# A hybrid HGRN2 and pooling decoder block in fp32: the order of the seven products of a pair, where the split operands begin, and the rooms of the pool's gates

## The chip, the core and the metric

The kernel runs on one core of a Trainium2 chip. Its five engines work side by side, each through its own list of instructions in order: TensorE (PE in the profile; its weight loads are listed apart as PEld), VectorE (DVE), ScalarE (ACT), GpSimd (POOL) and SyncE (SP), which here does nothing but issue transfers between DRAM and the on-chip memory. TensorE reads its two operands from the on-chip memory (SBUF) and writes its sums into eight accumulation banks (PSUM), from which VectorE and ScalarE read them. An instruction waits on semaphores for those of other engines that it depends on.

The metric is the device time of one execution in microseconds. Several executions of one kernel are given by their median. The profile is of one further execution; its span runs from the first to the last instruction.

## The reference

One decoder block over 1024 tokens of width 1024, all in fp32:

```python
def hybrid_mixer(x, w_in, lower_bound, hgrn_norm_g, w_a, w_pool, pool_scale, w_out):
    proj = x @ w_in                       # 1024 x 7168
    q, f_pre, i_val, o_gate, pool_v, gate_a, gate_b = jnp.split(proj, splits, axis=-1)
    ...
    o = hgrn2_chunked(q, 1 - f, i_val, log_f)        # 8 heads, a gated linear recurrence
    o = o * lax.rsqrt(jnp.mean(jnp.square(o), axis=-1, keepdims=True) + RMS_EPS)
    a = (o * hgrn_norm_g * jax.nn.sigmoid(o_gate)) @ w_a
    pooled = causal_multiscale_pool(pool_v)          # trailing means over 2, 4, 8, 16 tokens
    b = jnp.einsum('bsgc,gcd->bsgd', pooled, w_pool) * pool_scale
    merged = jax.nn.sigmoid(gate_a) * a + jax.nn.sigmoid(gate_b) * b
    return merged @ w_out

def sq_relu_mlp(x, w_up, w_down):
    return jnp.square(jax.nn.relu(x @ w_up)) @ w_down

x = layer_norm(ALPHA * x + hybrid_mixer(...));  x = layer_norm(ALPHA * x + sq_relu_mlp(x, w_up, w_down))
```

## The kernel before

**Three matmuls for one.** Every fp32 operand of a large product is split into a high part (rounded by a copy on ScalarE) and a low part (what is left, a subtraction on VectorE), and a product is the sum high x high + high x low + low x high: the three matmul lines 211, 213, 214 (and 112 to 114, 479 to 481, 1348 to 1350 in the other stages).

**Seven products for eight.** The products with w_in, w_a, w_up and w_down go through a scheme of Strassen and Winograd's kind. A *pair* (lines 266 to 353) is 256 output columns by 1024 tokens by 1024 deep, as 2 x 2 blocks b11, b12, b21, b22 of the weights. Seven operands are made from the blocks (b11, b21, T3 = b22 - b12, T4, T2, T1, b22), each is split into two w tiles (`w_part`, line 244, in lines 125 and 126; ring of ten, so five operands), and each meets one of seven activation operands that were split once and kept (`xp`: a11, a12, s3, a22, s2, s1, s4). A product is twelve matmuls of 128 x 512 (`prod`, line 206). Its sums go into banks: a takes P1, P6, P5, P3 one on top of the other; z takes P7, P4; c takes P2. Between these the sums so far are read: c11 = a after P1 (copied by ScalarE, line 274), c22 = z after P7, c21 = a after P6; P2 is added to c11, z (after P4) to c21, a (after P5) to c22 (VectorE, line 278), and a after P3 is the fourth block. `takes[0..3]` are what the pair's user does with the four results (sigmoid and store, pooling, squared ReLU). Ordinary banks are a ring of four (pj); z may lie in one of two others (hg, sc), c in tr.

**Order.** The steps of a pair stand in one tuple (line 350) as operand and product; `run` (line 357) makes the operands and issues the products of one pair, or of two pairs side by side (w_a, the first two pairs of w_up). With two side by side, a product of the one stands between two of the other; I call the others single pairs: 24 of w_in and 14 of w_up (the third of w_up has its first products among those of the two that run side by side). In the stage of w_in, from the pair after `head_inputs(0)` on, PE's order is the program's (`manual_schedule`, line 1016): after each product comes one step of the recurrence (`turning`, line 371), which is either nothing on PE, a few transposes and state products (lines 971, 937), or the large step of outputs, turned keys and scores (lines 955, 957, 894, 901, 912), once in 8.5 products. The other engines' order there, and every engine's elsewhere, is set when the program is built, by a planner that simulates the engines.

**Tiles.** Blocks of weights are loaded by SP (line 222, `loaded_blocks` line 230) into `raw`, a ring of six tiles, five for a pair of which "t" is scratch; results wait in `c` rooms (four on the left, two on the right). The tiles of the left side lie one behind another: constants (`const`, from line 134), two rings of statistics, then the 28 `act` tiles with the split activations, then `ca`. The w tiles, raw and two of the c rooms lie at the right end of the memory, where a filler of 96 bytes (line 82) sets where they begin, on a multiple of 128 bytes; with the sizes before them (const: ..., `prm` 128 bytes, `g_neg` 32, `lb` 32, `one_lb` 32, `e01` 64) the act tiles begin 32 bytes past one.

**Behind the recurrence** come four groups of `pool_products` (line 713: w_pool, its operands split into tiles of the tags q and f, four products each of six matmuls, a gate loaded for each from DRAM, multiplied in and stored again), the last gates, then w_a beside the loads of the recurrence's outputs, w_out, the first layer norm, w_up and w_down. Tags of the recurrence's rooms: q (three tiles), f (four), og (one), v (two).

Of the kernel before, what the change touches and what calls it, by code (L numbers as in the profile page):

```python
# [9 lines left out]
F32 = mybir.dt.float32  # L10
# [6 lines left out]
P = 128  # L17
# [3 lines left out]
KT = D // P  # L21
# [18 lines left out]
PRIO = 60  # L40
# [10 lines left out]
def tile_hybrid_block(  # L51
# [127 lines left out]
    def minus_sum(out, a, b):  # L179
        V.scalar_tensor_tensor(out, a, -1.0, b, ALU.mult, ALU.subtract)  # L180
# [25 lines left out]
    def prod(ps, w, name, first):  # L206
        wh, wl = w
        for k in range(CH):
            th, tl = xp[name][k][:, 0], xp[name][k][:, 1]
            with tc.high_priority(PRIO_WHOLE) if k else nullcontext():  # L210
                PE.matmul(ps, wh[:, k], th, start=first and k == 0, stop=False, skip_group_check=True)  # L211
            with tc.high_priority(PRIO_WHOLE):
                PE.matmul(ps, wh[:, k], tl, start=False, stop=False, skip_group_check=True)  # L213
                PE.matmul(ps, wl[:, k], th, start=False, stop=k == CH - 1, skip_group_check=True)  # L214
# [15 lines left out]
    def loaded_blocks(src, c1, c2, done=None):  # L230

        raw = {}
        for i in ((0, 0), (1, 0), (0, 1), "t", (1, 1)):
            raw[i] = block_tile(), None
            if i != "t":
                raw[i] = wide_block(src, i[0], (c1, c2)[i[1]], raw[i][0])
        if done is not None:
            done.append(raw[1, 1][1])
        return [raw[i][0] for i in ((0, 0), (0, 1), (1, 0), (1, 1), "t")]
# [4 lines left out]
    def w_part(src):  # L244
        return split(src, w_tile)
# [17 lines left out]
    def c_late():  # L263
        return c_tile(False)

    def pair(raw, rooms, takes, pz_tag="pj", pc_tag="pj", turned=False):


        b11, b12, b21, b22, t = raw if len(raw) == 5 else (*raw, None)
        c, ps = {}, {}  # L270

        def copied(room, ps):
            t = room()
            A.copy(t, ps)  # L274
            return t

        def added(t, ps):
            V.tensor_add(t, t, ps)  # L278
            return t

        def t3():
            c["t"] = block_tile() if t is None else t
            V.tensor_sub(c["t"], b22, b12)  # L283
            return w_part(c["t"])

        def t4():
            if turned:
                V.tensor_sub(b12, b11, b12)
                minus_sum(c["t"], b22, b12)
                minus_sum(b21, c["t"], b21)  # L290
            else:
                V.tensor_sub(b12, b12, b11)
                V.tensor_sub(c["t"], b22, b12)
                V.tensor_sub(b21, b21, c["t"])
            return w_part(b21)

        def t2():
            return w_part(c["t"])

        def t1():  # L300
            return w_part(b12)

        def p1(w):
            ps["a"] = ps_tile()
            prod(ps["a"], w, "a11", True)
            c[11] = copied(rooms[0], ps["a"])

        def p2(w):
            if pz_tag == "pj":
                ps["z"] = ps_tile()  # L310
            ps["c"] = ps_tile(pc_tag, 4 if pc_tag == "pj" else 2)
            prod(ps["c"], w, "a12", True)

        def p7(w):
            if pz_tag != "pj":
                ps["z"] = ps_tile(pz_tag, 2)
            prod(ps["z"], w, "s3", True)
            with tc.high_priority(PRIO):
                takes[0](added(c[11], ps["c"]))
                c[22] = copied(rooms[2], ps["z"])  # L320

        def p6(w):
            prod(ps["a"], w, "s2", False)
            with tc.high_priority(PRIO):
                c[21] = copied(rooms[1], ps["a"])
                takes[2](added(c[21], ps["z"]))

        def p4(w):
            prod(ps["z"], w, "a22", False)

        def p5(w):
            prod(ps["a"], w, "s1", False)
            with tc.high_priority(PRIO):
                takes[3](added(c[22], ps["a"]))

        def p3(w):
            prod(ps["a"], w, "s4", False)
            with tc.high_priority(PRIO):
                takes[1](ps["a"])

        def t0():
            return w_part(b11)

        def b_21():
            return w_part(b21)

        def b_22():
            return w_part(b22)

        return tuple(  # L350
            ((operand,), ((operand, product),))
            for operand, product in ((t0, p1), (b_21, p2), (t3, p7), (t4, p4), (t2, p6), (t1, p5), (b_22, p3))
        )

    turning = [iter(())]
# [46 lines left out]
    with tc.tile_pool(name="xr", bufs=8, side="right", reuse_waits="tile") as xr:  # L402
# [9 lines left out]
        PE.transpose(ps[:, 0:32], prm_r, ident[0:32, 0:32])  # L412
        V.tensor_copy(prm, ps[:, 0:32])
        g_col, pscale = prm[:, 16:24], prm[:, 24:32]
        g_neg = const.tile([P, 8], F32, name="g_neg")
        V.tensor_scalar_mul(g_neg, g_col, -1.0)
        lb = const.tile([P, 8], F32, name="lb")
        one_lb = const.tile([P, 8], F32, name="one_lb")
        e01 = const.tile([P, 16], F32, name="e01")
# [5 lines left out]
        V.reciprocal(lb, lb)  # L425
        V.tensor_mul(lb, lb, e01[:, 0:8])
        V.tensor_scalar(one_lb, lb, -1.0, 1.0, ALU.mult, ALU.add)
        x_rows = [xr.tile([P, CH, D], F32, name=f"x{u}", bufs=1) for u in range(2)]
        for t in range(8):
            r[t] = x_rows[t // CH][:, t % CH]  # L430
# [163 lines left out]
    def loaded(src, tile_of):  # L594
        t = tile_of()
        nc.sync.dma_start(out=t, in_=src)
        return t
# [25 lines left out]
    with tc.tile_pool(name="tmp", bufs=1, side="right", reuse_waits="tile") as tmp:  # L623
# [15 lines left out]
        def tt(tag, dtype=F32):  # L639
            pool = tmp if tag in ("q", "f", "og", "v") else hgp  # L640
            return pool.tile([P, HALF], dtype, tag=tag, name=nm(tag), bufs=RINGS.get(tag, 1))
# [70 lines left out]

        def pool_products(g):

            rooms = iter((lambda: tt("v"), c_tile, lambda: tt("f"), c_tile))
            raw = loaded(w_pool[g].rearrange("(k p) c -> p k c", p=P), lambda: block_tile((2, 2 * P)))
            pods = [[loaded(pod[2 * g + i][u], lambda: block_tile((HALF,))) for i in range(2)] for u in range(2)]
            parts = iter(("q", "f"))
            wh, wl = split(raw, lambda: tt(next(parts), F32R).rearrange("p (k c) -> p k c", c=2 * P))
            for u in range(2):  # L720
                pl = [split(pods[u][i], row_tile) for i in range(2)]
                for i in range(2):
                    w = slice(i * P, (i + 1) * P)
                    j = 2 * g + i
                    room = next(rooms)
                    t = room() if j == KT - 1 else loaded(gbd[j][u], room)
                    ps = ps_tile()
                    mm3(ps, [(wh[:, c, w], wl[:, c, w], *pl[c]) for c in range(2)])
                    if j == KT - 1:
                        A.activation(t, ps, AF.Copy, scale=pscale[:, j : j + 1])  # L730
                    else:
                        V.scalar_tensor_tensor(t, ps, pscale[:, j : j + 1], t, ALU.mult, ALU.mult)
                    nc.sync.dma_start(out=pbd[j][u], in_=t)
# [334 lines left out]
        def a_pair(p):  # L1068
            cols = 2 * p * P, (2 * p + 1) * P
            raw = loaded_blocks(w_a, *cols) if p in (0, 3) else wide_blocks(w_a, cols[0], mg_raw)  # L1070
            if p == 1:
                raw[0], _ = wide_block(w_a, 0, cols[0], block_tile())
            room = mg_tile("room", 4)
            takes = [gated(2 * p + i, u, p < 2) for u in range(2) for i in range(2)]
            return pair(raw, (c_tile, room, room), takes, "hg", turned=True)

        def unpark(*which):
            for u, j in which:
# [127 lines left out]
    with tc.tile_pool(name="up", bufs=1, side="right", reuse_waits="tile") as up:  # L1206
# [15 lines left out]
        def units(i, raw):  # L1222
            h = [None] * 4

            def put(slot, t):
                nc.sync.dma_start(out=hid[i][slot], in_=t)

            def take(n):
                def take(src):
                    h[n] = relu2(c_tile() if n == 1 else src, src)  # L1230
                return take

            def last(src):
                take(1)(src)
                h11, h12, h21, h22 = h
                s1 = c_tile()
                V.tensor_add(s1, h21, h22)
                put(4, s1)
                put(3, h22)
                V.tensor_sub(h21, h11, h21)  # L1240
                put(5, h21)
                put(0, h11)
                s2 = c_tile()
                V.tensor_sub(s2, s1, h11)
                put(2, s2)
                s4 = c_tile()
                V.tensor_sub(s4, h12, s2)
                put(1, h12)
                put(6, s4)

            return pair(raw, (c_tile,) * 3, (take(0), last, take(2), take(3)), "hg", "tr" if i == 2 else "pj")

        blocks = loaded_blocks(w_up, 0, P), wide_blocks(w_up, 2 * P, up_raw_tile)
        pairs = [units(i, raw) for i, raw in enumerate(blocks)]
# [212 lines left out]
```

## Time and profile before

| | us |
|---|---|
| median of three runs (lowest, highest) | 1571.11 (1570.29, 1572.27) |
| the profiled execution, own time | 1568.92 |
| its span | 1567.2 |
| PE busy | 1479.0 |
| DVE busy | 1105.1 |
| ACT busy | 761.3 |

| stretch, us | what runs there | PE busy, us | DVE busy, us |
|---|---|---|---|
| 0 to 99 | values (w_in's third part), by rows | 92.88 | 70.36 |
| 99 to 715 | single pairs of w_in, with the recurrence | 549.17 | 406.10 |
| 715 to 738 | w_pool | 22.53 | 17.81 |
| 738 to 850 | last gates, w_a | 106.55 | 93.40 |
| 850 to 930 | w_out, first norm | 80.00 | 47.64 |
| 930 to 1262 | w_up | 332.00 | 227.70 |
| 1262 to 1567 | w_down, second norm | 295.83 | 242.11 |

A row of the profile that begins with a line number is a group of instructions: engine, operation, what it writes and reads by the program's names, count, busy time and mean duration, then the engine's idle time before them and who ended it. Matmuls overlap: one of 128 x 512 is shown as some 390 ns long, though the next starts some 230 ns after it. "ACT c L274" as a releaser means that the wait ended when ScalarE had made a `c` tile in line 274.

### The profile page before, as it was taken

How to read it: one execution, taken by the hardware profiler on the slowest of the kernel's cores; microseconds unless marked ns; L12 is line 12 of the kernel's file. 1: busy time of each engine (PE TensorE's matmuls, PEld its weight loads, DVE VectorE, ACT ScalarE, POOL GpSimd, SP SyncE). 2: the span in 40 equal slices, each digit the busy share in tenths (PEclk: the TensorE clock that was granted, in tenths of full speed). 3: DMA queues.
4: the chain of work that ended last, by engine and by line, in shares of the span. 5: the costliest groups of instructions: out<-in, count | busy, mean ns of one | idle time of the engine just before them, and what ended most of it. 6: DMA issues, size and time to landing. Idle time of an engine off the chain costs nothing.

```text
span 1567.2 us, 20891 instructions
## 1 busy us (share of the span) xinstructions
PE 1479.0 (94%) x7377; PEld 1189.9 (76%) x7377; DVE 1105.1 (71%) x1807; ACT 761.3 (49%) x1383; POOL 106.4 (7%) x288
## 2 busy tenths in 40 slices
PE   8998988888999899899999999999999999999997
PEld 7786776666777677677778888888888888888886
DVE  4967765585678569546898559756666777777978
ACT  5444454445655455444554237655555633333445
POOL 0002101101111111000000210000000000000000
PEclk9999999999999999999999999999999999999999
DMA  7132134333334443469866312544446594535322
GB/s 247 61 123 81 55 94 142 92 110 94 128 92 103 116 108 89 120 173 351 295 205 224 108 67 82 179 149 148 148 148 245 190 331 135 197 119 188 126 77 108
DMA packets 187738, 229.21 MB, mean 146 GB/s; under 512 B 12240, under 2 KB 110576, under 8 KB 187632
## 3 DMA queue, kind: packets, MB, share of 16 engines
q1 hardware_dynamic: 181664, 213.96, 40.9%
q0 software_dynamic: 5184, 11.54, 3.8%
q10 hardware_dynamic: 784, 2.38, 0.5%
q8 instruction: 58, 0.95, 0.2%
q14 instruction: 48, 0.39, 0.1%
HBM read 150.22 MB, written 77.59 MB: 145 GB/s over the span
## 4 chain that ended last, share of the span: by engine, by line
PE 54%; DMA 2%; DVE 2%; ACT 1%; issue 0%; DVEq 0%; ACTq 0%; SPq 0%
PE ps_pj L211 7%; PE ps_pj L214 7%; PE ps_pj L213 7%; PE ps_pj L1348 4%; PE ps_pj L1350 4%; PE ps_pj L1349 4%; PE ps_pj L113 2%; PE ps_pj L114 2%; PE ps_pj L112 2%; PE ps_tr L1348 1%; PE ps_tr L1350 1%; PE ps_tr L1349 1%; PE ps_hg L211 1%; PE ps_sc L211 1%; PE ps_hg L213 1%; PE ps_sc L213 1%
## 5 line engine op out<-in xcount | busy, mean ns | idle before, releaser
L211 PE MATMUL ps_pj<-act,w 128*128 128x512 f32 x1068 | 434.8, 407 | 69.7 <-ACT c L274 34.5
L214 PE MATMUL ps_pj<-act,w 128*128 128x512 f32 x1068 | 424.1, 398 | 1.2 <-DVE w L126 1.2
L213 PE MATMUL ps_pj<-act,w 128*128 128x512 f32 x1068 | 423.8, 398 | 0.1
L125 ACT CAST w<-raw 128x512 fp32r<-128x512 f32 x327 | 202.0, 621 | 386.6 <-PE ps_pj L213 281.7
L126 DVE TENSOR_TENSOR w<-raw,w 128x512 fp32r<-128x512 f32 x327 | 223.9, 688 | 212.2 <-ACT w L125 209.9
L211 PEld LDWEIGHTS ps_pj<-act,w 128*128 128x128 f32 x1068 | 202.2, 189 | 140.4 <-ACT c L274 47.3
L214 PEld LDWEIGHTS ps_pj<-act,w 128*128 128x128 f32 x1068 | 202.3, 189 | 51.5 <-DVE w L126 2.0
L213 PEld LDWEIGHTS ps_pj<-act,w 128*128 128x128 f32 x1068 | 202.9, 190 | 45.9 <-DVE act L131 0.6
L1310 ACT CAST act<-act 128x1024 fp32r<-128x1024 f32 x66 | 67.1, 1050 | 108.5 <-issue 35.0
L1349 PE MATMUL ps_pj<-act,act 128*128 128x512 f32 x240 | 93.0, 389 | 0.0
L1350 PE MATMUL ps_pj<-act,act 128*128 128x512 f32 x240 | 93.0, 389 | 0.0
L1348 PE MATMUL ps_pj<-act,act 128*128 128x512 f32 x240 | 92.4, 389 | 0.0
L1311 DVE TENSOR_TENSOR act<-act,act 128x1024 fp32r<-128x1024 f32 x66 | 79.4, 1221 | 15.0 <-ACT act L1310 15.0
L278 DVE TENSOR_TENSOR c<-c,ps_pj 128x512 f32<-128x512 f32 x95 | 64.9, 683 | 31.3 <-PE ps_pj L214 30.3
L274 ACT COPY c<-ps_pj 128x512 f32<-128x512 f32 x96 | 55.8, 581 | 5.0 <-PE ps_pj L214 3.3
L1350 PEld LDWEIGHTS ps_pj<-act,act 128*128 128x128 f32 x240 | 45.0, 188 | 9.4
L1349 PEld LDWEIGHTS ps_pj<-act,act 128*128 128x128 f32 x240 | 45.0, 188 | 9.3
L1348 PEld LDWEIGHTS ps_pj<-act,act 128*128 128x128 f32 x240 | 45.0, 188 | 9.3
L283 DVE TENSOR_TENSOR raw<-raw,raw 128x512 f32<-128x512 f32 x43 | 29.6, 689 | 20.8 <-DMA raw<-in_w_in_dram 18.9
L1219 ACT ACTIVATE c<-c 128x512 f32<-128x512 f32 x61 | 38.5, 633 | 1.5
L1218 ACT ACTIVATE c<-c 128x512 f32<-128x512 f32 x46 | 29.1, 632 | 13.8 <-DVE c L278 13.6
L618 POOL DMA_DIRECT2D s<-og x28 | 24.9, 1162 | 145.8 <-DVE og L973 145.8
(410 smaller groups left out, 2668.2 us busy)
## 6 DMA issues: line engine op xcount, KB each, us to landing
h<-c SPq DMA_DIRECT2D x106, 256.0 KB, 2.8
raw<-in_w_in_dram SPq DMA_DIRECT2D x100, 256.0 KB, 3.1
act<-h SPq DMA_DIRECT2D x78, 256.0 KB, 2.9
draw<-in_w_down_dram SPq DMA_DIRECT2D x16, 1024.0 KB, 7.5
raw<-in_w_up_dram SPq DMA_DIRECT2D x56, 256.0 KB, 2.9
hf<-h SPq DMA_DIRECT2D x34, 256.0 KB, 2.9
s<-og POOLq DMA_DIRECT2D x28, 256.0 KB, 6.1
v<-v SPq DMA_DIRECT2D x16, 256.0 KB, 3.0
```

Of the source, the lines that this page charges most:

```text
L125: A.copy(hi, src)
L126: V.tensor_sub(lo, src, f(hi))
L211: PE.matmul(ps, wh[:, k], th, start=first and k == 0, stop=False, skip_group_check=True)
L213: PE.matmul(ps, wh[:, k], tl, start=False, stop=False, skip_group_check=True)
L214: PE.matmul(ps, wl[:, k], th, start=False, stop=k == CH - 1, skip_group_check=True)
L274: A.copy(t, ps)
L278: V.tensor_add(t, t, ps)
L1310: A.copy(hi, src)
L1311: V.tensor_sub(lo, src, f(hi))
L1348: PE.matmul(ps, hh[:, w], wh, start=fresh and n == 0, stop=False, skip_group_check=True)
L1349: PE.matmul(ps, hh[:, w], wl, start=False, stop=False, skip_group_check=True)
L1350: PE.matmul(ps, hl[:, w], wh, start=False, stop=n == M - 1, skip_group_check=True)
```

## The change

The single pairs' products run as P1, P2, P6, P7, P5, P4, P3; pairs that run two side by side keep P1, P2, P7, P4, P6, P5, P3 (`twin`). For this T2 is made early and in b11's tile, T3 keeps t; in a single pair the first of the three middle operands makes T3, T1 and T2 together. In a single pair takes[2] comes behind P4 rather than P6. `loaded_blocks` takes the scratch tile of the ring before b12's. `g_neg` no longer has a tile of its own but the first half of `e01`. In `pool_products` the rooms of the four gates of a group are v, q, f, og instead of v, c, f, c.

```diff
@@ -230,7 +230,7 @@
     def loaded_blocks(src, c1, c2, done=None):
 
         raw = {}
-        for i in ((0, 0), (1, 0), (0, 1), "t", (1, 1)):
+        for i in ((0, 0), (1, 0), "t", (0, 1), (1, 1)):
             raw[i] = block_tile(), None
             if i != "t":
                 raw[i] = wide_block(src, i[0], (c1, c2)[i[1]], raw[i][0])
@@ -263,7 +263,7 @@
     def c_late():
         return c_tile(False)
 
-    def pair(raw, rooms, takes, pz_tag="pj", pc_tag="pj", turned=False):
+    def pair(raw, rooms, takes, pz_tag="pj", twin=False, pc_tag="pj", turned=False):
 
 
         b11, b12, b21, b22, t = raw if len(raw) == 5 else (*raw, None)
@@ -278,24 +278,37 @@
             V.tensor_add(t, t, ps)
             return t
 
-        def t3():
+        def make_t3():
             c["t"] = block_tile() if t is None else t
             V.tensor_sub(c["t"], b22, b12)
-            return w_part(c["t"])
-
-        def t4():
+
+        def make_t2():
             if turned:
                 V.tensor_sub(b12, b11, b12)
-                minus_sum(c["t"], b22, b12)
-                minus_sum(b21, c["t"], b21)
+                minus_sum(b11, b22, b12)
             else:
                 V.tensor_sub(b12, b12, b11)
-                V.tensor_sub(c["t"], b22, b12)
-                V.tensor_sub(b21, b21, c["t"])
+                V.tensor_sub(b11, b22, b12)
+
+        def t3():
+            if twin:
+                make_t3()
+            return w_part(c["t"])
+
+        def t2():
+            if not twin:
+                make_t3()
+                make_t2()
+            return w_part(b11)
+
+        def t4():
+            if twin:
+                make_t2()
+            if turned:
+                minus_sum(b21, b11, b21)
+            else:
+                V.tensor_sub(b21, b21, b11)
             return w_part(b21)
-
-        def t2():
-            return w_part(c["t"])
 
         def t1():
             return w_part(b12)
@@ -323,10 +336,14 @@
             prod(ps["a"], w, "s2", False)
             with tc.high_priority(PRIO):
                 c[21] = copied(rooms[1], ps["a"])
-                takes[2](added(c[21], ps["z"]))
+                if twin:
+                    takes[2](added(c[21], ps["z"]))
 
         def p4(w):
             prod(ps["z"], w, "a22", False)
+            if not twin:
+                with tc.high_priority(PRIO):
+                    takes[2](added(c[21], ps["z"]))
 
         def p5(w):
             prod(ps["a"], w, "s1", False)
@@ -347,9 +364,11 @@
         def b_22():
             return w_part(b22)
 
+        middle = (
+            ((t3, p7), (t4, p4), (t2, p6), (t1, p5)) if twin else ((t2, p6), (t3, p7), (t1, p5), (t4, p4))
+        )
         return tuple(
-            ((operand,), ((operand, product),))
-            for operand, product in ((t0, p1), (b_21, p2), (t3, p7), (t4, p4), (t2, p6), (t1, p5), (b_22, p3))
+            ((operand,), ((operand, product),)) for operand, product in ((t0, p1), (b_21, p2), *middle, (b_22, p3))
         )
 
     turning = [iter(())]
@@ -412,8 +431,6 @@
         PE.transpose(ps[:, 0:32], prm_r, ident[0:32, 0:32])
         V.tensor_copy(prm, ps[:, 0:32])
         g_col, pscale = prm[:, 16:24], prm[:, 24:32]
-        g_neg = const.tile([P, 8], F32, name="g_neg")
-        V.tensor_scalar_mul(g_neg, g_col, -1.0)
         lb = const.tile([P, 8], F32, name="lb")
         one_lb = const.tile([P, 8], F32, name="one_lb")
         e01 = const.tile([P, 16], F32, name="e01")
@@ -425,6 +442,8 @@
         V.reciprocal(lb, lb)
         V.tensor_mul(lb, lb, e01[:, 0:8])
         V.tensor_scalar(one_lb, lb, -1.0, 1.0, ALU.mult, ALU.add)
+        g_neg = e01[:, 0:8]
+        V.tensor_scalar_mul(g_neg, g_col, -1.0)
         x_rows = [xr.tile([P, CH, D], F32, name=f"x{u}", bufs=1) for u in range(2)]
         for t in range(8):
             r[t] = x_rows[t // CH][:, t % CH]
@@ -712,7 +731,7 @@
 
         def pool_products(g):
 
-            rooms = iter((lambda: tt("v"), c_tile, lambda: tt("f"), c_tile))
+            rooms = iter(("v", "q", "f", "og"))
             raw = loaded(w_pool[g].rearrange("(k p) c -> p k c", p=P), lambda: block_tile((2, 2 * P)))
             pods = [[loaded(pod[2 * g + i][u], lambda: block_tile((HALF,))) for i in range(2)] for u in range(2)]
             parts = iter(("q", "f"))
@@ -722,8 +741,8 @@
                 for i in range(2):
                     w = slice(i * P, (i + 1) * P)
                     j = 2 * g + i
-                    room = next(rooms)
-                    t = room() if j == KT - 1 else loaded(gbd[j][u], room)
+                    tag = next(rooms)
+                    t = tt(tag) if j == KT - 1 else loaded(gbd[j][u], lambda: tt(tag))
                     ps = ps_tile()
                     mm3(ps, [(wh[:, c, w], wl[:, c, w], *pl[c]) for c in range(2)])
                     if j == KT - 1:
@@ -1072,7 +1091,7 @@
                 raw[0], _ = wide_block(w_a, 0, cols[0], block_tile())
             room = mg_tile("room", 4)
             takes = [gated(2 * p + i, u, p < 2) for u in range(2) for i in range(2)]
-            return pair(raw, (c_tile, room, room), takes, "hg", turned=True)
+            return pair(raw, (c_tile, room, room), takes, "hg", True, turned=True)
 
         def unpark(*which):
             for u, j in which:
@@ -1248,7 +1267,7 @@
                 put(1, h12)
                 put(6, s4)
 
-            return pair(raw, (c_tile,) * 3, (take(0), last, take(2), take(3)), "hg", "tr" if i == 2 else "pj")
+            return pair(raw, (c_tile,) * 3, (take(0), last, take(2), take(3)), "hg", i < 2, "tr" if i == 2 else "pj")
 
         blocks = loaded_blocks(w_up, 0, P), wide_blocks(w_up, 2 * P, up_raw_tile)
         pairs = [units(i, raw) for i, raw in enumerate(blocks)]
```

## The prediction

> **What bounds the kernel now.** I read the engine shares first, then the busy time by stage, then who waits for whom in the stage that has gaps, then the order of time around single gaps.
>
> ```profile
> span 1567.2 us, 20891 instructions
> PE 1479.0 (94%) x7377; PEld 1189.9 (76%) x7377; DVE 1105.1 (71%) x1807; ACT 761.3 (49%) x1383; POOL 106.4 (7%) x288
> ```
>
> TensorE (PE) is the bound, with 88 us in which it does nothing. The stages tell where these lie (columns: stretch, length, PE busy with its instructions, granted clock, DMA share, GB/s):
>
> ```profile
> 118.80:715.30 596.50, 529.67 (x3217) 0.98 0.39 111
> 1010.00:1240.00 230.00, 230.00 (x988) 1.00 0.49 168
> 1270.00:1440.00 170.00, 170.00 (x751) 1.00 0.53 180
> ```
>
> From 1010 to 1440 us PE never stops. The 596.5 us from 118.8, in which 22 single pairs and the recurrence run in an order of PE written out by hand, hold 66.8 us of the idle time. Nearly all of it has one line and four releasers (us in total, times, longest):
>
> ```profile
> PE ps_pj L211 <- ACT c L274: 34.5, 30, 2.9
> PE ps_pj L211 <- DVE c L278: 13.5, 11, 2.6
> PE ps_pj L211 <- ACT f L274: 10.0, 6, 4.0
> PE ps_pj L211 <- DVE f L278: 8.8, 6, 3.3
> ```
>
> L211 is the first matmul of a product, L274 the copy out of a bank, L278 the addition out of a bank. So PE stands 53 times before a product, until somebody has read the bank that it is to write. In the pair of 586 to 611 us it is these three:
>
> ```profile
> 594.69 0.40 PE L214 MATMUL ps_pj<-act,w 128*128 128x512 f32 x1
> 596.04 0.50 PE L211 MATMUL ps_pj<-act,w 128*128 128x512 f32 x1 [0.96 <-ACT c L274]
> 596.38 0.39 PE L213 MATMUL ps_pj<-act,w 128*128 128x512 f32 x1
> ...
> 603.96 0.50 PE L211 MATMUL ps_pj<-act,w 128*128 128x512 f32 x1 [0.96 <-ACT c L274]
> ...
> 607.79 0.50 PE L211 MATMUL ps_pj<-act,w 128*128 128x512 f32 x1 [0.78 <-DVE c L278]
> ```
>
> They are the starts of P4 (bank z right after P7, whose copy is wanted first), P5 (bank a right after P6) and P3 (bank a right after P5): in the order P1, P2, P7, P4, P6, P5, P3 three neighbours write the same bank. Of 66 such places in 22 pairs 53 show idle time; in the others a step of the recurrence happened to stand between.
>
> **The change: order of the products.** In P1, P2, P6, P7, P5, P4, P3 the banks go a, c, a, z, a, z, a: a reader always has one product of another bank, twelve matmuls, to finish in. What is removed, on the path: the idle time, 66.8 us; at each of the 53 places also what idle does not count: from 594.69 to 596.04 and on to 596.38 it is 1.69 us for two steps that take 0.23 each elsewhere, 1.23 lost where 0.96 is shown, so 0.27 more each, 14.3 us; and slow matmuls after the longest gaps:
>
> ```profile
> 295.41 0.50 PE L211 MATMUL ps_pj<-act,w 128*128 128x512 f32 x1 [3.95 <-ACT f L274]
> ...
> 296.44 0.63 PE L211 MATMUL ps_pj<-act,w 128*128 128x512 f32 x1
> 296.86 0.63 PE L213 MATMUL ps_pj<-act,w 128*128 128x512 f32 x1
> ...
> L213 PE MATMUL ps_pj<-act,w 128*128 128x512 f32 x616 | 246.4, 400 | 0.0
> ```
>
> Behind that gap matmuls follow at 0.42 instead of 0.23. In this stage L213 means 400 ns where its median is 394 to 396 (below): some 5 ns on 616, at 0.237 above the median each, are 13 slow ones, so about 39 over the three lines; at 0.19 lost each this is 7.5 us. Together 66.8 + 14.3 + 7.5 = 89 us. These are covered by a product of twelve times 0.23, 2.7 us, against a smallest need of 0.96 + 0.27; so a reader may be 1.5 us later than it must be before PE waits again.
>
> What stays: the four longest waits above 2.7 - 0.27 keep 0.5 + 0.2 + 1.6 + 0.9, 3 us, as the lower end. P6 is new as a waiter: it had P2, P7 and P4 between itself and the copy of P1, now P2 alone. And the readers' engines get denser, as the same work falls into some 505 us (596.5 - 89 + 10, and 12 for 1848 matmuls by the part on starts). They are what is late next. DVE is the tighter one (columns PE, PEld, DVE, ACT, POOL, then clock, DMA share, GB/s):
>
> ```profile
> 550.00:650.00 100.00, 89.72 (x574) 71.56 (x573) 77.97 (x165) 51.98 (x118) 17.34 (x44) 1.00 0.41 110
> ...
> 594.33 0.69 DVE L126 TENSOR_TENSOR w<-raw,w 128x512 fp32r<-128x512 f32 x1
> 594.93 0.69 DVE L292 TENSOR_TENSOR raw<-raw,raw 128x512 f32<-128x512 f32 x1
> ```
>
> Passes of 0.69 follow each other at 0.60, so 78 us busy are 68 us of its time; in 85 us that is 80%, ACT 61%. That leaves room on the mean, not at each place. Upper end: the slack is overrun so often that half of what is waited now comes back, 33 us. Below nothing the cost can't go, since 89 is all the time that stands there. I take 10, near the lower end, because the dense stages run with one product between reader and writer and show no idle.
>
> Edits with no price: takes[2] moves behind P4, with its addition on DVE, its sigmoid on ACT and its store on SP, past takes[0] and takes[3] and their stores (P3 and the next P1 still lie before its bank is written again, and nobody reads the stored gate within the pair); P7's operand comes fourth, T2 is built in b11 instead of t; the subtractions stay four per pair, made up to five operands ahead (ten w tiles), which is the cover. Where that is gone it is one pass, 0.69, per product.
>
> **The moved loads.** b21 of the next pair now takes the buffer of this pair's b11, last read by the sixth operand instead of the fourth, and SP's loads of b12 and b22 stand behind it. What waits for them is the second and third operand.
>
> ```profile
> SPq L222 <- DVE w L126: 290.3, 94, 17.8
> ...
> raw<-in_w_in_dram SPq DMA_DIRECT2D x100, 256.0 KB, 3.1
> ...
> L283 DVE TENSOR_TENSOR raw<-raw,raw 128x512 f32<-128x512 f32 x43 | 29.6, 689 | 20.8 <-DMA raw<-in_w_in_dram 18.9
> L125 ACT CAST w<-raw 128x512 fp32r<-128x512 f32 x327 | 202.0, 621 | 386.6 <-PE ps_pj L213 281.7
> ```
>
> The loop from sixth operand to sixth operand: landing 3.1, issue 0.4, four operands at 0.62 + 0.69, four subtractions at 0.69: 11.5 us, against 22.9 us of PE per pair (505 / 22). Hidden; nothing.
>
> **Operands on 128 bytes.** Without g_neg's own 32 bytes the constants before the activation tiles shrink by 32, and act tiles (32 bytes past a multiple of 128 so far, from the sizes of the tiles before them) begin on it, as the weight tiles at the other end already do. Matmul durations by the tiles they read (minimum, median, maximum):
>
> ```profile
> L213 PE MATMUL ps_pj<-act,w x1068: 389/394/632, 99.4 to 1261.9; 128*128 128x512 f32 x178
> ...
> L112 PE MATMUL ps_pj<-act,act x80: 389/389/478, 832.8 to 932.3; 128*128 128x512 f32 x80
> L112 PE MATMUL ps_pj<-w,q x32: 387/389/494, 715.4 to 737.9; 128*128 128x512 f32 x32
> L112 PE MATMUL ps_pj<-wo,act x32: 392/396/397, 868.5 to 935.1; 128*128 128x512 f32 x32
> L112 PE MATMUL ps_pj<-w,act x16: 395/396/397, 865.7 to 930.9; 128*128 128x512 f32 x16
> ...
> L480 PE MATMUL ps_pj<-w,act x64: 392/396/628, 13.4 to 98.7; 128*128 128x512 f32 x64
> ```
>
> One and the same line L112 takes 389 where both operands begin alike (both act, or w and q, both on 128) and 396 where they differ. The spacing agrees: 230 us / 988 = 233 ns in the single pairs of w_up, 170 / 751 = 226 where both are act. So 6.4 ns on each mixed matmul: three lines of 1232 (1068 for bank pj, the rest in other banks), three of 112 around L480, 144 in the output product: 4176 x 6.4 = 27 us, all where PE is dense or becomes so. Ends: 0 (the 7 ns have another cause; a loss is excluded, as no row with equal starts has the larger median) and 27, which I take, since the four pairs of operands of L112 all fall on the right side of it.
> The page "SBUF — State Buffer" of the Trainium skill (section "SBUF: two separate sides") gives TensorE its own ports, the weight load included, and says that it never waits for anyone there; by that the start of a tile would change nothing, and the sum would be 27 higher. The medians 389 and 396 speak against it, though no row here shows the start changed alone.
>
> **Rooms of w_pool's gates.** Two of four gates per group leave the six c rooms for q (three) and og (one).
>
> ```profile
> 725.00:738.00 13.00, 12.53 (x53) 9.47 (x52) 9.58 (x15) 4.99 (x9) 0.00 (x0) 1.00 1.03 370
> 760.00:850.00 90.00, 85.52 (x362) 67.31 (x362) 77.56 (x127) 44.25 (x79) 0.00 (x0) 1.00 0.64 212
> ...
> pb<-c SPq DMA_DIRECT2D x8, 256.0 KB, 5.3
> ...
> f<-gb SPq DMA_DIRECT2D x3, 256.0 KB, 5.6
> ```
>
> DMA is full there. One og room means load 5.6, pass 0.7, store 5.3, one after another: 11.6 us per group, where PE needs 23 / 4 = 5.8. DVE stops at the late gate, and behind it stand the splits that PE needs: at most 3 x 5.8 = 17 us. The other end is -5: the freed c rooms let the first operands of w_a come sooner, and 760 to 850 us has 4.5 us idle. I take +4, as the landings shorten once PE waits.
>
> **Sum.** 1567.2 - 89 + 10 - 27 + 4 = 1465 span; 1.7 outside it (1568.92 against 1567.2) makes 1467, and the median of the runs shown is 2.2 above that one: **1469 us**, own range 1451 (1469 - 7 with only 3 kept, - 9 with -5 for the rooms, - 2 for the spread of the runs, 1570.29 to 1572.27) to 1485.
>
> **Rivals.**
> Starts don't matter: 1469 + 27 = 1496. For it: no mixed pair of tiles begins alike in this trace, and mixed tiles also lie at opposite ends of memory. Chance 0.10.
> Readers late: DVE and ACT, denser, give back 33 us and not 10: 1469 + 23 = 1492. For it: the copy behind the 3.95 us at 295.41 was 3 us late already in the looser stage; against it: 80% and 61% leave room. 0.10.
> The new order doesn't do what it says: the copies are late by more than a product, and only 10 of 89 us go: 1548. Against: 0.96 is by far the commonest gap. 0.05.
> Slower: the load of b21 at the head of SP's queue. Each time it stands there for the longest wait, 17.8, the loop is 11.5 + 17.8 = 29.3 us; it decides from 22.9 us on. Over 22 pairs (29.3 - 22.9) x 22 = 141, so 1610. Against: 290.3 us over 94 waits are 3.1 on the mean. 0.03.
>
> **Chances.** Forecast 0.72, rivals 0.28 as given. The range 1451 to 1502 holds the first three (1496 with a few us to spare). A measurement of this kernel tells 0.2%, 3 us, from nothing: faster 0.96, same 0.01, slower 0.03.
>
> **What would show it.** Right: no idle at P4, P5, P3 beyond 10 us in the single pairs, their stage near 505 us; act,w medians 389 and some 440 matmuls per 100 us in the pairs of w_up; the down product unchanged. Wrong: waits of L211 for L274 or L278 that stay above 20 us; act,w still at 396; PE idle from 715 us on with DVE waiting for gb; loads into raw whose landing DVE waits for at L283.

## The result and the profile after

| | before | after |
|---|---|---|
| median, us (four runs each) | 1570.93 | 1473.64 |
| lowest, highest | 1570.29, 1572.27 | 1472.62, 1474.58 |
| span of the profiled execution | 1567.2 | 1470.8 |

The ratio is 0.938, with a 95% interval from 0.9363 to 0.9396. The prediction was 1469 us, 1451 to 1502.

The engine shares of the changed kernel:

```profile
span 1470.8 us, 20899 instructions
PE 1438.0 (98%) x7377; PEld 1189.8 (81%) x7377; DVE 1100.2 (75%) x1807; ACT 760.8 (52%) x1383; POOL 107.4 (7%) x288
```

PE has 33 us without work instead of 88, and its own busy time fell by 41 us with the same 7377 matmuls. The stretches that answer to those shown of before (the 22 single pairs with the recurrence, w_pool, dense pairs of w_up, the down product; length, PE busy with its instructions, granted clock, DMA share, GB/s):

```profile
116.90:620.20 503.30, 497.88 (x3217) 1.00 0.46 128
620.20:651.40 31.20, 26.23 (x98) 0.89 1.07 395
880.00:1110.00 230.00, 230.00 (x1016) 1.00 0.47 159
1180.00:1350.00 170.00, 170.00 (x752) 1.00 0.52 176
```

The same 3217 matmuls of the single pairs took 596.5 us before. 230 us of w_up hold 1016 matmuls where they held 988; the down product is as it was (752 against 751). All waits of PE in the first of these stretches (total, times, longest) are these, where 66.8 us in 53 places were before:

```profile
PE ps_pj L211 <- ACT c L274: 2.9, 2, 1.5
PE ps_pj L211 <- DVE f L278: 1.2, 1, 1.2
PE ps_pj L211 <- ACT f L274: 1.1, 1, 1.1
```

And the matmul durations by operands, minimum, median, maximum:

```profile
L213 PE MATMUL ps_pj<-act,w x1068: 387/389/628, 98.0 to 1164.1; 128*128 128x512 f32 x178
...
L112 PE MATMUL ps_pj<-w,q x32: 389/389/628, 620.3 to 650.8; 128*128 128x512 f32 x32
...
L112 PE MATMUL ps_pj<-wo,act x32: 389/389/476, 777.9 to 843.5; 128*128 128x512 f32 x32
...
L112 PE MATMUL ps_pj<-w,act x16: 389/389/389, 775.2 to 839.4; 128*128 128x512 f32 x16
```

Every pair of operands now has the median 389. Before, act,w in this line L213 had 394, and w,act and wo,act 396.

One stage became longer: w_pool, 31.1 us instead of 23.5, with the granted clock at 0.89 and DMA full. First the stage before, then after (here PE, PEld, DVE, ACT, POOL, then clock, DMA share, GB/s):

```profile
715.00:738.50 23.50, 23.03 (x99) 18.12 (x98) 17.81 (x27) 10.88 (x18) 0.00 (x0) 1.00 0.97 345
...
620.20:651.30 31.10, 26.13 (x98) 19.65 (x97) 19.68 (x29) 11.01 (x18) 0.00 (x0) 0.89 1.07 395
```

So some 8 us of the gain are given back there, and a part of them comes back behind it. How much shows in a longer stretch, from the first matmul of w_pool to the first of w_up, which holds the same work in every kernel (w_pool, the last gates, w_a, w_out). Before and after:

```profile
715.40:935.80 220.40, 214.48 (x933) 171.23 (x932) 160.62 (x263) 94.44 (x163) 14.42 (x6) 1.00 0.59 202
...
620.30:844.20 223.90, 214.99 (x934) 174.54 (x933) 160.68 (x263) 95.32 (x163) 14.38 (x6) 0.98 0.60 207
```

At w_up 3.5 us of the 8 are left. Why, the experiments had to tell.

### The profile page after: what moved, and what is told of

Its sections match the earlier page's. It is cut to its first block, busy times and chain, and to the rows that moved or that the text cites. A ratio compares the mean times of both kernels' runs of the same rounds, so it can differ in the third digit from the quotient of the medians.

```text
span 1470.8 us, 20899 instructions
## 1 busy us (share of the span) xinstructions
PE 1438.0 (98%) x7377; PEld 1189.8 (81%) x7377; DVE 1100.2 (75%) x1807; ACT 760.8 (52%) x1383; POOL 107.4 (7%) x288
## 4 chain that ended last, share of the span: by engine, by line
PE 88%; DVE 5%; DMA 4%; issue 1%; ACT 1%; SPq 0%; POOL 0%; DVEq 0%; ACTq 0%
PE ps_pj L211 15%; PE ps_pj L214 15%; PE ps_pj L213 15%; PE ps_pj L1369 4%; PE ps_pj L1367 4%; PE ps_pj L1368 4%; PE ps_pj L112 2%; PE ps_pj L113 2%; PE ps_pj L114 2%; PE ps_tr L1369 1%; PE ps_tr L1367 1%; PE ps_tr L1368 1%; PE ps_sc L211 1%; PE ps_sc L213 1%; PE ps_sc L214 1%
## 5 line engine op out<-in xcount | busy, mean ns | idle before, releaser
L211 PE MATMUL ps_pj<-act,w 128*128 128x512 f32 x1068 | 420.5, 394 | 8.3 <-ACT c L274 2.9
L214 PE MATMUL ps_pj<-act,w 128*128 128x512 f32 x1068 | 416.0, 391 | 2.3 <-DVE w L126 2.3
L213 PE MATMUL ps_pj<-act,w 128*128 128x512 f32 x1068 | 415.3, 390 | 0.0
L213 PEld LDWEIGHTS ps_pj<-act,w 128*128 128x128 f32 x1068 | 201.0, 188 | 40.5
L283 DVE TENSOR_TENSOR raw<-raw,raw 128x512 f32<-128x512 f32 x43 | 29.6, 689 | 28.2 <-DMA raw<-in_w_in_dram 27.1
L1323 DVE TENSOR_TENSOR act<-act,ps_pj 128x512 f32<-128x512 f32 x45 | 30.1, 681 | 6.0 <-PE ps_pj L1369 5.7
```

## The experiments

The theory: three terms that add up, the order (79 us), the starts (27 us), the rooms (-4 us). Its rivals: the starts don't matter, or the multiple of 128 is what counts; readers that are late; the rooms' chain or the full DMA for the stage of w_pool.

**1. The order alone**, on the kernel before. Against the changed kernel that is:

```diff
+        g_neg = const.tile([P, 8], F32, name="g_neg")
...
-        g_neg = e01[:, 0:8]
...
-            rooms = iter(("v", "q", "f", "og"))
+            rooms = iter((lambda: tt("v"), c_tile, lambda: tt("f"), c_tile))
```

> The new order of the products alone, on the kernel before (g_neg keeps its tile, the gates of w_pool keep their c rooms). Theory (terms of the prediction add up): 89 us of stalls go and about 10 stay, so 1571 - 79 = 1492 us, some 0.950 of before; L211 idle under 15 us in the single pairs, act,w median still 396 ns. Rival (most of the gain is the starts): over 1530 us.

Measured: 1491.89 us against 1571.47 of the kernel before on the same chip, ratio 0.949 (0.9474 to 0.9506): 79.6 us. Its waits and its two stretches:

```profile
117.90:630.10 512.20, 507.78 (x3217) 1.00 0.45 126
880.00:1110.00 230.00, 230.00 (x988) 1.00 0.43 146
...
PE ps_pj L211 <- ACT c L274: 2.5, 2, 1.3
PE ps_pj L211 <- DVE f L278: 1.2, 1, 1.2
PE ps_pj L211 <- ACT f L274: 0.7, 1, 0.7
```

The single pairs go from 596.5 to 512.2 us with matmuls as slow as before (988 in 230 us). The waits for the readers of a bank are gone but for 4.4 us, and this part is the larger by far.

**2. The starts alone**, on the kernel before:

```diff
-        g_neg = const.tile([P, 8], F32, name="g_neg")
-        V.tensor_scalar_mul(g_neg, g_col, -1.0)
...
+        g_neg = e01[:, 0:8]
+        V.tensor_scalar_mul(g_neg, g_col, -1.0)
```

> g_neg in e01 alone, on the kernel before: act tiles begin on 128 bytes, order and rooms as before. Theory: 4176 mixed matmuls at 6.4 ns, 27 us, and the 53 waits of L211 stay at some 67 us: 1544 us, 0.983 of before; act,w median 389 ns. Rival (the 7 ns have another cause, as that mixed tiles lie at opposite ends of memory): 1571 us, median 396.

Measured: 1554.69 us, 0.9896 (0.9879 to 0.9913), 16.8 us: neither of the two. The matmuls do what the theory says, PE does not gain as much:

```profile
L213 PE MATMUL ps_pj<-act,w x1068: 387/389/632, 98.8 to 1250.6; 128*128 128x512 f32 x178
...
117.60:711.90 594.30, 524.28 (x3218) 0.98 0.40 111
1010.00:1240.00 230.00, 230.00 (x1017) 1.00 0.51 174
```

In w_up, where PE is dense, 1017 matmuls instead of 988 stand in 230 us, 6.6 ns each, the forecast term. In the single pairs only 2.2 us of some 12 came (594.3 against 596.5). PE is idle there for 70.0 us instead of 66.8: a product that ends sooner waits longer for a reader whose own work got no shorter. And by the trace's record of the granted clock PE stands at half clock for 27.3 us there instead of 20.5, which costs up to 3.4 us more. Some 3 us stay open; this profile is also the slowest of the four executions, 2.9 us above their median. That the tiles lie at opposite ends of memory is ruled out as the cause: they still do, and the median is 389.

**3. and 4. The rooms undone, and a c room for og alone**, on the changed kernel:

```diff
-            rooms = iter(("v", "q", "f", "og"))
+            rooms = iter((lambda: tt("v"), c_tile, lambda: tt("f"), c_tile))        # 3
+            rooms = iter((lambda: tt("v"), lambda: tt("q"), lambda: tt("f"), c_tile))  # 4
```

> The changed kernel with the gates of w_pool in v, c, f, c again. Theory (one og room serialises load, pass and store): the stage of w_pool goes from 31 back to 23 us and the whole to about 1466 us, 0.995 of the changed kernel. Rival (the rooms pay, the longer stage has its cause in DMA that is full): no shorter stage, 1473 us or more, with more idle time before the first products of w_a.

> The changed kernel with only the fourth gate of each group in a c room in place of og (v, q, f, c). Theory (og's single room is what holds): the stage of w_pool near 23 to 25 us, the whole about 1467 us. Rival (not og but q's ring of three, which the split weights share, or the full DMA): the stage stays at 30 us and the whole at 1473 us.

Measured: 1473.54 us (0.9378, 0.9361 to 0.9395) and 1473.8 us (0.9377, 0.9358 to 0.9395). The stage of w_pool is shorter in both, but neither kernel is measurably faster than the changed one, 0.938. Run 3, the stage and then the longer stretch:

```profile
621.60:648.10 26.50, 24.05 (x97) 17.44 (x96) 17.48 (x27) 10.60 (x18) 0.00 (x0) 1.00 1.04 378
621.60:842.80 221.20, 211.72 (x934) 171.27 (x933) 159.78 (x263) 94.58 (x163) 14.38 (x6) 1.00 0.62 211
```

The stage takes 26.5 us where the changed kernel has 31.1 and the kernel before 23.5; to w_up it is 221.2, 223.9 and 220.4. So the rooms cost some 4.6 us in their stage, and by w_up 2.7 of them are left. The other 3 us of the longer stage are there with the rooms as before too. They came with the order: the stage takes 26.5 us in run 1 and 22.8 in run 2. The 2.7 us are about as much as the intervals allow (0.17% either way, 2.6 us), and the medians don't show them: the changed kernel came out at 0.938 and, in run 11 below, at 0.9394. Run 4, in its stage:

```profile
619.80:646.90 27.10, 23.26 (x97) 17.45 (x96) 18.91 (x29) 10.84 (x18) 0.00 (x0) 1.00 1.05 378
```

With og's room alone given up most of the rooms' 4.6 us comes back in the stage, but the total does not move. That alone would still fit the chain of og; run 9 below has og's room and the short stage.

Runs 1 and 3 differ in the starts alone: 1491.89 against 1473.54 on one chip, 18.4 us. The single pairs show again what is lost of it:

```profile
114.30:621.60 507.30, 499.61 (x3218) 1.00 0.45 126
```

507.3 after 512.2 us, with 7.7 us idle after 4.4: 4.9 us of 12. One profile doesn't fix this number: the changed kernel and runs 3, 4, 5, 8, 9 and 11, whose single pairs are the same, have 503.3 to 508.3 us there, so 4 to 9 us of the 12 came.

**5. and 6. Both ends moved by 32 bytes; the act tiles moved by 64**, on the changed kernel:

```diff
-    G.memset(pad.tile([P, 24], F32, name="pad_top"), 0.0)
+    G.memset(pad.tile([P, 16], F32, name="pad_top"), 0.0)      # 5, with g_neg's own tile again
...
+        G.memset(const.tile([P, 16], F32, name="shift"), 0.0)  # 6
```

> The changed kernel with both ends moved: act tiles begin 32 bytes past a multiple of 128 as before, and the filler at the right end is 64 bytes instead of 96, so w, raw, q, f, v and og begin 32 past one too. Theory (what counts is that the two operands of a matmul begin alike): act,w median 389 ns, 1474 us as the changed kernel. Rival (what counts is the multiple of 128 itself): act,w 396 ns or more, 1490 us, and the down product, act,act, stays at 389.

> The changed kernel with 64 bytes of unused constants, so act tiles begin 64 past a multiple of 128 and w tiles on one. Theory (the two have to begin alike within 128 bytes): act,w median 396 ns and about 1491 us. Rival (within 64 bytes is enough): 389 ns and 1474 us.

Measured: 1475.92 us (0.9384, 0.9367 to 0.94) for 5, as the changed kernel; 1483.28 us (0.9431, 0.9417 to 0.9445) for 6. In run 5:

```profile
L213 PE MATMUL ps_pj<-act,w x1068: 387/389/628, 97.5 to 1166.2; 128*128 128x512 f32 x178
```

No large tile begins on 128 bytes there, and the median is 389: it is the two operands that have to begin alike. In run 6:

```profile
L213 PE MATMUL ps_pj<-act,w x1068: 387/392/628, 99.0 to 1175.3; 128*128 128x512 f32 x178
...
L112 PE MATMUL ps_pj<-w,act x16: 394/394/394, 782.4 to 847.6; 128*128 128x512 f32 x16
...
890.00:1120.00 230.00, 230.00 (x1006) 1.00 0.46 157
```

1006 matmuls in 230 us lie between 988 and 1016: 64 bytes apart cost, but less than 32. Neither of the two expectations had that. On the same chip run 6 is 7.4 us slower than run 5.

**7. One pair of neighbours left**, on the changed kernel, in the order P1, P2, P7, P6, P4, P5, P3:

```diff
...
-            ((t3, p7), (t4, p4), (t2, p6), (t1, p5)) if twin else ((t2, p6), (t3, p7), (t1, p5), (t4, p4))
+            ((t3, p7), (t4, p4), (t2, p6), (t1, p5)) if twin else ((t3, p7), (t2, p6), (t4, p4), (t1, p5))
```

> The changed kernel with the single pairs in the order P1, P2, P7, P6, P4, P5, P3: banks a, c, z, a, z, a, a, so that P5 and P3 alone are neighbours in one bank. Theory (each such place costs what it cost before): the waits of L211 for L278 come back, 22 us in 17 places and 0.27 more each, so some 25 us: 1499 us. Rival (a wait removed at one place comes out at the next, since VectorE is what is late): under 1482 us.

In this run T3 is made with P7's operand again, as the order needs it. Measured: 1507.83 us (0.9588, 0.9565 to 0.9612), 32 us over run 5 on the same chip, which is as fast as the changed kernel. The waits for VectorE, and those alone, are back:

```profile
PE ps_pj L211 <- DVE c L278: 15.2, 13, 3.9
PE ps_pj L211 <- DVE f L278: 12.3, 6, 4.1
...
117.40:657.10 539.70, 509.58 (x3215) 0.98 0.43 121
```

27.5 us in 19 places, 0.27 more each, and a granted clock of 0.98 in place of 1.00 (17.1 us at half clock, up to 8.5 us lost): the stretch is 36 us longer (539.7 against 503.3). So this kind of place costs on its own, and more than it was forecast to: the waits are longer than the 22.3 us that they took before, and the expectation had left the slow clock out. The two other kinds were not put back alone.

**8. w_pool's operands not loaded**, on the changed kernel:

```diff
-            pods = [[loaded(pod[2 * g + i][u], lambda: block_tile((HALF,))) for i in range(2)] for u in range(2)]
+            pods = [[block_tile((HALF,)) for _ in range(2)] for _ in range(2)]
+            for u in range(2):
+                for i in range(2):
+                    G.memset(pods[u][i], 0.5)
```

> The changed kernel in which w_pool's operands are not loaded but set to 0.5 by GpSimd: the output lacks the pooled values, and 16 transfers of 256 KB fall away in the stage of w_pool. Theory (the DMA engines, full there, hold the stage at 31 us): the stage goes to 22 to 24 us and the whole to about 1464 us. Rival (the rooms' chain of load, pass and store, or the late splits, hold it): 28 us or more there, 1471 us or more.

Measured: 1471.7 us (0.9355, 0.9337 to 0.9374). The stage went to 26.0 us, between the two expectations, with PE busy for 24.0:

```profile
623.40:649.40 26.00, 24.01 (x97) 18.85 (x96) 18.44 (x28) 10.73 (x18) 3.69 (x7) 0.93 0.92 306
```

The loads are a part of what holds the stage. The whole is 4.2 us below run 5 on the same chip, about what the stage lost; this run also has GpSimd fill the tiles, which no run separates. What the changed kernel's ScalarE waits for in that stage, and SP's list at its begin:

```profile
ACT w L125 <- DMA raw<-po: 10.5, 7, 3.3
...
617.86 0.32 SPq L615 DMA_DIRECT2D c<-o  x1
618.27 0.38 SPq L615 DMA_DIRECT2D raw<-po  x1
...
623.03 0.32 SPq L615 DMA_DIRECT2D c<-o  x1
...
625.74 0.32 SPq L615 DMA_DIRECT2D c<-o  x1
626.63 0.38 SPq L615 DMA_DIRECT2D raw<-po  x1
627.06 0.45 SPq L615 DMA_DIRECT2D c<-o  x1
```

The freed c rooms let the first operand of w_a (c<-o), wanted in the next stage, go between the loads that w_pool wants now (raw<-po), with DMA full. In the kernel before, the first of these loads stands behind the last of those:

```profile
729.66 0.32 SPq L596 DMA_DIRECT2D raw<-po  x1
...
738.54 0.32 SPq L596 DMA_DIRECT2D c<-o  x1
```

That gave the next run.

**9. The first operand of w_a behind w_pool's last load**, on the changed kernel; **10.** the ring's order of before in `loaded_blocks`; **11.** the changed kernel once more, on the same chip:

```diff
+                    last_pod[:] = [nc.sync.dma_start(out=pods[u][i], in_=pod[2 * g + i][u]).ins]   # 9
...
-        o_operand("a11")
+        with tc.issue_after(last_pod[0]):
+            o_operand("a11")                                   # 9
...
-        for i in ((0, 0), (1, 0), "t", (0, 1), (1, 1)):
+        for i in ((0, 0), (1, 0), (0, 1), "t", (1, 1)):        # 10
```

> The changed kernel with the first activation operand of w_a (the loads c<-o) issued only behind the last load of w_pool's operands (raw<-po). Theory (the freed c rooms let c<-o go first through a full DMA, and ScalarE waits 10.5 us for raw<-po): the stage of w_pool goes from 31 to 24 to 27 us; the first products of w_a may wait 0 to 3 us more; 1468 to 1471 us, 0.997 of the changed kernel on the same chip. Rival (the DMA is full either way): the stage stays at 29 us or more, or what it gains is waited for in w_a; within 0.2% of the changed kernel.

> The changed kernel with the ring's order of before in the loads of a pair's blocks (b12's tile before the scratch tile), so that b12 takes the buffer that the sixth operand frees, and not the fourth. Theory (the moved loads are hidden, 11.5 us against 22.9): within 0.2% of the changed kernel. Rival (SP's queue is near the bound): 5 us or more slower, with VectorE waiting over 40 us for raw at L283 in place of 27.

> The changed kernel itself once more, to compare the other two of this call on one chip: 1474 us within 3 us, 0.938 of before.

Measured: 9 has 1471.94 us (1470.72 to 1472.72; 0.9362, 0.9345 to 0.9379), 11 has 1476.74 us (1475.41 to 1478.16; 0.9394, 0.9376 to 0.9411), 10 has 1475.33 us (0.9387, 0.9369 to 0.9405). Run 9 is 4.8 us faster than the changed kernel beside it, its slowest execution faster than that one's fastest, and so faster than the kernels before and after the change; the intervals of the two ratios touch (0.9379 and 0.9376). Its stage of w_pool, and the longer stretch:

```profile
624.20:650.20 26.00, 23.48 (x97) 19.04 (x96) 18.73 (x28) 10.81 (x18) 0.00 (x0) 0.93 1.06 381
624.20:844.40 220.20, 212.63 (x934) 173.99 (x933) 160.79 (x263) 95.32 (x163) 14.38 (x6) 0.98 0.61 209
...
ACT w L125 <- DMA raw<-po: 4.2, 3, 2.7
```

The stage takes 26.0 us instead of 31.2 in run 11, with the DMA share at 1.06 against 1.07, and to w_up it is 220.2 us instead of 224.6. ScalarE waits 4.2 us for raw<-po; in the changed kernel it was 10.5, in run 11 8.7. So it is the order of the loads, at nearly the same DMA share, that made the stage longer with the new rooms, and not the one room og, which run 9 keeps. Run 10 has the ring's order of before, which moves the loads of b12 and b22: it is within 0.1% of run 11, and VectorE waits as long for raw (30.6 us there, 29.3 in run 11, by the waits of L283). No run puts b21's load back where it was.

## Why the prediction was right

The whole: 102 us of gain forecast, 97.3 measured. The time lies this near for a mixed reason: the order's term came out, the term of the starts was some 9 us too large, and the 4 us set against the gain for the rooms are not to be seen in the medians, which evens out a part of it.

*The bound and the place of the gain.* 66.8 us of idle time at P4, P5 and P3: right. Run 1 removes them and gives 79.6 us, against 89 - 10 = 79. That these agree to a microsecond is in part luck: the single pairs alone became 84.3 us shorter, as 4.4 us stayed and not 10, and w_pool, which had no term for it, gave 3 us back. Run 7 shows that one of the three kinds of place, P3 behind P5, costs on its own. The length of the single pairs was given as 505 us; it is 503.3, and 507.5 in the second profile of the same kernel.

*What would stay.* 10 us were left for readers that are still late; 5.2 us of idle time stayed, in four places, though the same work of VectorE now fills 78% of the stretch (392.0 us busy of 503.3) instead of 66% (395.8 of 596.5). One product of another bank was cover enough, as the dense stages had suggested; the rival "readers late" falls. The prediction gives no sum for the upper end of its own range, 1485; with its own 33 us for late readers it would have been 1492, which the wider range holds.

*The starts.* The price of a matmul was right, 6.4 ns (1016 against 988 in 230 us), and so was the cause. The term of the sum was too large: 27 us on paper, 16.8 us alone and 18.4 us on top of the order. The step that failed is "all where PE is dense or becomes so". It holds in w_up, where 16 pairs, 1344 matmuls, take 317.7 us in run 2 instead of 326.3: 6.4 ns each. In the single pairs, 12 us of the term, run 2 shows 2.2 us, and in the new order 4 to 9 us came. In the old order PE runs on until the next late reader: 3.2 us more of idle time and up to 3.4 us more at half clock. In the new order run 3 has 3.3 us more of idle time than run 1; few gaps did not make the stage one that PE alone sets. What else is lost there is not split up further.
The page "SBUF — State Buffer" of the Trainium skill (section "SBUF: two separate sides") would have had the starts do nothing, since TensorE reads through its own ports. The measurement decides against that reading: run 2, in which the starts alone change, moves the median from 394 to 389 and the time by 16.8 us. By what way a start costs time, no run shows.

*The rooms.* +4 us were taken, between -5 and 17; the medians show no difference that is clear of noise, while the traces have 2.7 us at w_up. The mechanism named, one og room that serialises load, pass and store, is not what decides: run 9 has that room, and its stage is as short (26.0 us) as that of run 3 without it (26.5). What holds the stage instead is the place in the DMA queue of loads that the freed rooms admit, and run 9 moves those. The term was near by its size and wrong in its mechanism, which is luck. The 3 us by which the stage grew with the rooms as before (26.5 us in runs 1 and 3 against 23.5) had no term in the sum. They come with the order; the pairs ahead are 15% shorter and leave less time for w_pool's loads, which run 8 makes likely but does not prove.

*Moved loads and the slower rival.* Free, as far as the runs tell: the waits of PE that are left in the single pairs all name the reader of a bank, none a weight operand, and run 10 doesn't change the time. VectorE's waits for raw grew from 18.9 to 27.1 us (29.3 in run 11), and PE does not see them.

## What to carry to other kernels

Where products are summed onto one accumulation bank and read in between, order them so that a product of another bank stands between writer and reader, and count the gap with the restart and the slow clock behind it (0.27 us and up to 1.7 us here), not by the idle time alone. Look at which tiles a matmul reads, not only at its shape: the same line ran at two speeds by where its operands begin. A term that is a price per instruction holds in the stages that this engine bounds; elsewhere multiply it by less, and after a gain look where the transfers of the next stage now stand in the queue.

## What the runs showed of the hardware

A matmul of 128 x 512 in fp32 halves has a spacing that depends on how far apart its two operands begin within 128 bytes: 230 us / 1016 = 226 ns where they begin alike, 230 / 988 = 233 ns at 32 bytes, 230 / 1006 = 229 ns at 64 bytes. Both 32 past a multiple of 128 is as good as both on one (run 5). Other distances, 128 bytes itself among them, were not run.

The clock fell to half behind short gaps. In the changed kernel's stage of w_pool:

```profile
633.55 0.54 PE L112 MATMUL ps_pj<-w,q 128*128 128x512 f32 x1 [2.24 <-ACT q L125]
633.89 0.63 PE L113 MATMUL ps_pj<-w,q 128*128 128x512 f32 x1
...
636.57 0.63 PE L113 MATMUL ps_pj<-w,q 128*128 128x512 f32 x1
...
637.36 0.40 PE L112 MATMUL ps_pj<-w,q 128*128 128x512 f32 x1
```

2.24 us without work, after a dense stretch, were followed by some 3.4 us of matmuls at 0.42 us each. So a gap of 2.2 us cost its own length and some 1.7 us more (nine steps in 3.81 us, from 633.55 to 637.36, instead of in 2.07). The page "TensorE: Matmul & The Clock Gate" of the Trainium skill (section "What's actually happening") lets the clock fall after an idle window of about 3.4 us and come back after as long a busy one; the trace agrees with the second, while here 2.24 us were enough for the first.
The traces' record of the granted clock shows more: it changes only in steps of 3.41 us, and a fall goes with the idle time that lies within one step. In the kernel before, all seven stretches at half clock ahead of the last norm follow a step in which PE was idle for 1.92 us or more. A gap of 2.22 us, ended at 156.29 us, with 1.92 of it in one step, was followed by half clock; a longer one, 2.85 us, ended at 649.15 us, that lay 1.21 and 1.64 us in two steps, was not.
